# A hybrid backbone on one core: the end of layer 0 and the start of layer 1 done by token segments

## The chip, the core and the metric

The kernel runs on one core of a Trainium2 chip. The metric is device time in microseconds (us), the median of several executions. A core has a matrix engine (TensorE, PE in the profile; its weight loads are shown as PEld), a vector engine (VectorE, DVE), a scalar engine that evaluates functions (ScalarE, ACT), GpSimd (POOL) and a queue that issues transfers (SyncE, SP). Each engine works through its own list of instructions strictly in order and stops at an instruction whose inputs are not there.

## What is computed

The network is a two-layer trunk over 256 context tokens and 512 latent tokens with 1024 channels. Each layer has a normalised and modulated input, a mixer, and then a gated convolutional feed-forward network (FFN). Cut to what matters:

```python
def trunk_layer(x_lat, x_ctx, c, c_ctx, p, mixer, rope, need_ctx):
    m_lat = [m[:, None, :] for m in adaln_mods(c, p)]
    m_ctx = adaln_mods(c_ctx, p)
    o_ctx, o_lat = mixer(modulate(x_ctx, p['norm_mix_g'], m_ctx[0], m_ctx[1]),
                         modulate(x_lat, p['norm_mix_g'], m_lat[0], m_lat[1]), p, rope, need_ctx)
    x_lat = x_lat + m_lat[2] * o_lat
    x_lat = x_lat + m_lat[5] * conv_ffn(modulate(x_lat, p['norm_ffn_g'], m_lat[3], m_lat[4]), p)
    ...

def conv_ffn(h, p):
    u = dwconv_centred(h @ p['ffn_w_up'], p['ffn_conv_w'], p['ffn_conv_b'])
    gate, val = jnp.split(u, 2, axis=-1)
    return (jax.nn.silu(gate) * val) @ p['ffn_w_down']
```

`modulate` is an RMS norm over the 1024 channels of one token, times a gain and a scale, plus a shift. Layer 1's mixer is a Mamba-2 state-space part (`ssd`) beside windowed attention. Its input projection makes, among others, the 32 decay columns (`dt`) and the columns B and C (`bm`, `cm`), which go through a five-tap convolution and a silu.

## The kernel before, in words

Channels lie on the 128 partitions and tokens along the free axis, so an activation of all tokens is eight tiles of 128 x 768: 256 context columns and then 512 latent ones. `SEG2` lists the two segments, context first; the two token groups have different modulation, so every residual and every modulation is written per segment.

Every product is made in three passes to keep precision: a weight tile is split into a rounded high half (`whi`, a cast on ScalarE, line 325) and a low half (`wlo`, a subtraction on VectorE, or on GpSimd for the layer-1 input weights, line 326), the activation into `hi` and `lo` likewise, and `dense` adds hi*hi, lo*hi and hi*lo in one accumulator. One weight tile serves one output block of 128 channels. Raw weights arrive in two buffers (`NWR` = 2), the halves are kept in three (`NW` = 3): a raw buffer is loaded again once the low half of its tile is made, and a pair of halves is overwritten once the product that used it is done. `plan` lists all weight tiles in the order of use.

The FFN of layer 0 runs over four groups of hidden blocks (6, 6, 5, 5). For each group the `up` products make the hidden blocks, and then eight `down` products, one per output block `m` and here 5 blocks x 3 passes x 2 segments = 30 matmuls each, are added into the residual tiles `x` by `resid` (VectorE, line 484). After the last group comes layer 1's norm, `prenorm`: `sumsq` squares each `x` tile (ScalarE, line 429), adds the squares of tiles 0 to 6 on GpSimd (line 434), and sums over the partitions with a product by a matrix of ones; `rstd` makes the inverse root with Ln and Exp (lines 415 and 416, one function-table load in front of each); then, for each tile, u = x * gain * r (VectorE, line 462), the high half (ScalarE, line 463) and the low half (VectorE, line 477, for five tiles; lines 469 and 474 on ScalarE and GpSimd for the last three). The latents of `x` are also saved to memory (`sp_x`). Then `ada_group` (64 small matmuls for a later modulation), `decays` (the `dt` columns, a chain of functions and scans, a store `sp_ac` and its reload `E`, spread over all partitions), the two B blocks (dense, five-tap convolution, silu at line 1237, transposes at line 1243), the two C blocks (accumulator `sd`), and so on. `decays` and the first B block use the `by_pass` order: all eight hi*hi matmuls first, then lo*hi, then hi*lo.

The program is written tile by tile; a list scheduler then sets a fixed order for each engine, by its own costs and by the pools that tiles are taken from. What stands in those lists is therefore not the order of the text.

## Time and profile before

| What | us |
|---|---|
| Median of 3 runs (lowest, highest) | 2268.85 (2264.03, 2269.86) |
| The profiled execution's own time | 2264.21 |
| Its span, first to last instruction | 2262.3 |
| PE busy | 2076.5 (92%) |
| DVE busy | 1346.3 (60%) |
| ACT busy | 928.3 (41%) |
| POOL busy | 506.2 (22%) |

The shares are averages over stages with different limits, so the table only says that TensorE is the engine to follow. The stretch that the change touches lies between 1336 us, where the last eight down products of layer 0 begin, and about 1440 us, where TensorE takes up the transposes of the first B block; the views below are cut to it. In a row of the timeline stand the start, the length, engine, line, operation, output<-inputs, shapes and count, and in brackets the idle time before and what ended it. The three runs differ by 0.26%.

### The profile page before, as it was taken

To read this page: it belongs to the slowest core of one execution; us is meant where nothing else is said; L and a number is where in the kernel's file an instruction comes from. 1 tells how busy PE (TensorE), PEld (TensorE's weight loads), DVE (VectorE), ACT (ScalarE), POOL (GpSimd) and SP (SyncE) were. 2 spreads that over 40 slices of the span, in tenths; PEclk is the share of its full clock that TensorE was granted. 3 is DMA by queue.
4 is the path that set the end of the run, shared out by engine and by line. 5 is a ranking of instruction groups with operands and counts; after the bars stand their busy time and mean duration, and the time that the engine had idled before them with its cause. 6 is when DMAs were issued, how large, how long until landed. Compare 5 with 4: busy or idle time off the path is not lost.

```text
span 2262.3 us, 33884 instructions
## 1 busy us (share of the span) xinstructions
PE 2076.5 (92%) x13558; PEld 1640.9 (73%) x13558; DVE 1346.3 (60%) x2081; ACT 928.3 (41%) x1434; POOL 506.2 (22%) x486
## 2 busy tenths in 40 slices
PE   5888889788998999999999998898888999999997
PEld 3666667566654878888888886786565667888886
DVE  5566965666766465445354444678985556554555
ACT  4445663532355244233132335544344345342434
POOL 0027686611223010000000004442641230000000
PEclk9999999698999999999999999999889999999998
DMA  8477777669741441211212213213426032323231
GB/s 303 125 206 206 182 211 195 211 190 320 259 165 42 154 139 62 61 66 57 75 53 60 75 58 114 96 52 117 133 71 172 28 111 79 96 92 98 84 116 61
DMA packets 181069, 282.58 MB, mean 125 GB/s; under 512 B 63328, under 2 KB 118656, under 8 KB 177840
## 3 DMA queue, kind: packets, MB, share of 16 engines
q1 hardware_dynamic: 180912, 280.42, 40.6%
q8 instruction: 107, 1.75, 0.3%
q14 instruction: 50, 0.41, 0.1%
HBM read 225.43 MB, written 47.33 MB: 121 GB/s over the span
## 4 chain that ended last, share of the span: by engine, by line
PE 65%; DVE 6%; ACT 5%; DMA 5%; issue 3%; POOL 1%; SPq 0%; DVEq 0%; ACTq 0%; POOLq 0%
PE acc L267 49%; PE sd L267 3%; PE o L267 3%; PE wo L267 2%; PE ab L267 2%; PE b L267 2%; DMA u<-sp_v 1%; DVE E L1359 1%; DMA aw<-ada 1%; POOL I L750 1%; PE ax L267 1%; PE ad L267 1%; POOL w L748 1%; DMA E<-sp_ac 1%; ACT L416 1%
## 5 line engine op out<-in xcount | busy, mean ns | idle before, releaser
L267 PE MATMUL acc<-s,whi 128*128 128x512 f32 (+1 forms) x3104 | 759.8, 356 | 3.0 <-ACT s L463 3.0
L267 PEld LDWEIGHTS acc<-s,whi 128*128 128x128 f32 x3104 | 546.0, 188 | 97.3 <-ACT s L463 4.8
L267 PE MATMUL acc<-s,wlo 128*128 128x512 f32 (+1 forms) x1552 | 462.0, 358 | 0.0
L267 PE MATMUL acc<-h,whi 128*128 128x256 f32 (+2 forms) x1248 | 321.1, 371 | 15.9 <-ACT p L639 5.0
L325 ACT CAST whi<-wraw 128x1024 fp32r<-128x1024 f32 (+5 forms) x228 | 210.0, 923 | 282.3 <-PE acc L267 218.0
L267 PEld LDWEIGHTS acc<-s,wlo 128*128 128x128 f32 x1552 | 289.5, 188 | 42.9 <-DVE wlo L326 0.7
L267 PEld LDWEIGHTS acc<-h,whi 128*128 128x128 f32 (+1 forms) x1248 | 223.7, 197 | 68.4 <-issue 15.4
L326 DVE TENSOR_TENSOR wlo<-wraw,whi 128x1024 fp32r<-128x1024 f32 (+5 forms) x205 | 218.7, 1069 | 44.2 <-ACT whi L325 43.6
L381 DVE SCALAR_TENSOR_TENSOR s<-acc,pv,s 128x511 f32<-128x511 f32 (+1 forms) x132 | 87.0, 659 | 246.2 <-ACT s L380 245.4
L380 ACT ACTIVATE s<-acc,pv 128x512 f32<-128x512 f32 (+1 forms) x132 | 93.4, 708 | 235.4 <-PE acc L267 224.2
L484 DVE SCALAR_TENSOR_TENSOR x<-acc,mods,x 128x512 f32<-128x512 f32 (+1 forms) x136 | 79.4, 620 | 175.0 <-PE acc L267 174.8
L267 PE MATMUL acc<-h,wlo 128*128 128x256 f32 (+2 forms) x624 | 179.5, 362 | 0.0
L434 POOL TENSOR_TENSOR f<-f,f 128x768 f32<-128x768 f32 (+1 forms) x24 | 31.3, 1306 | 635.0 <-ACT f L429 625.1
L267 PEld LDWEIGHTS acc<-h,wlo 128*128 128x128 f32 (+1 forms) x624 | 119.3, 195 | 21.9 <-issue 5.6
L1178 POOL TENSOR_TENSOR s<-w,s 128x256 f32<-128x256 f32 x6 | 5.0, 855 | 381.3 <-ACT s L416 381.3
L383 DVE SCALAR_TENSOR_TENSOR s<-acc,pv,s 128x511 f32<-128x511 f32 (+1 forms) x132 | 87.2, 660 | 4.2
L750 POOL TENSOR_TENSOR I<-I,w 128x30 f32<-128x30 f32 (+14 forms) x120 | 76.7, 639 | 9.0
L748 POOL TENSOR_TENSOR w<-I 128x30 f32<-128x30 f32 (+14 forms) x120 | 69.4, 578 | 34.6 <-PE iv L267 25.8
L387 ACT CAST s<-s 128x768 fp32r<-128x768 f32 (+1 forms) x44 | 32.0, 727 | 106.1 <-DVE s L1151 106.1
L326 POOL TENSOR_TENSOR wlo<-wraw,whi 128x1024 fp32r<-128x1024 f32 x23 | 61.7, 2686 | 59.6 <-ACT whi L325 56.1
L1359 DVE TENSOR_SCALAR E<-E,acm 128x128 f32<-128x128 f32 x128 | 61.2, 546 | 14.6 <-ACT G L1356 14.6
L723 DVE TENSOR_TENSOR W<-gk,con 64x512 f32<-64x512 f32 x48 | 32.8, 683 | 51.2 <-ACT PB L722 47.3
(390 smaller groups left out, 3347.3 us busy)
## 6 DMA issues: line engine op xcount, KB each, us to landing
aw<-ada SPq DMA_DIRECT2D x96, 512.0 KB, 5.8
wraw<-up SPq DMA_DIRECT2D x88, 512.0 KB, 3.5
rec<-sp_rec SPq DMA_DIRECT2D x24, 1024.0 KB, 9.7
wraw<-w_in SPq DMA_DIRECT2D x47, 512.0 KB, 3.8
wraw<-down SPq DMA_DIRECT2D x40, 384.0 KB, 3.1
...
E<-sp_ac SPq DMA_DIRECT2D x16, 512.0 KB, 5.5
...
```

Of the source, the lines that this page charges most:

```text
L267: ins = nc.tensor.matmul(o, lhsT=lhsT, rhs=rhs, start=start, stop=stop, skip_group_check=shared)
L325: nc.scalar.copy(hi[:, :kt], raw[:, :kt])
L326: (eng or tt)(out=lo[:, :kt], in0=raw[:, :kt], in1=hi[:, :kt].bitcast(F32), op=ALU.subtract)
L380: act(o[rows, t0:t0 + n], ps[rows, po:po + n], AF.Identity, scale=w1, bias=b)
L381: stt(out=o[rows, t0 + 1:t0 + n], in0=ps[rows, po:po + n - 1], scalar=w0, in1=o[rows, t0 + 1:t0 + n], op0=ALU.mult, op1=ALU.add)
L383: stt(out=o[rows, t0:t0 + n - 1], in0=ps[rows, po + 1:po + n], scalar=w2, in1=o[rows, t0:t0 + n - 1], op0=ALU.mult, op1=ALU.add)
L387: nc.scalar.copy(hi, src)
L484: stt(out=x[:, t0:t0 + n], in0=ps[:, po:po + n], scalar=mods[:, c6 * 8 + m, c:c + 1], in1=x[:, t0:t0 + n], op0=ALU.mult, op1=ALU.add)
L723: tt(out=w[hk], in0=b[hk].rearrange("p c (a t) -> p c a t", a=2), in1=mk[hk].rearrange("p (a t) -> p a t", a=2).unsqueeze(1).to_broadcast( ...
L748: eng.tensor_tensor(out=tmp, in0=I[:, m + 1:, m:m + 1].to_broadcast([P, n, m]), in1=I[:, m:m + 1, :m].to_broadcast([P, n, m]), op=ALU.mult)
L750: eng.tensor_tensor(out=I[:, m + 1:, :m], in0=I[:, m + 1:, :m], in1=tmp, op=ALU.add)
L1359: ts(out=e[:, h], in0=e[:, h], scalar1=acm[:, c, h0 + h:h0 + h + 1], scalar2=0.0, op0=ALU.subtract, op1=ALU.min)
```

## The change

Only the end of layer 0 and the start of layer 1 are written differently.

- In the last group of layer 0's FFN the eight down products are made for the latents alone, then layer 1's norm of the latents is written (`tail`), then the eight down products for the context, and the norm of the context. Each of the eight weight tiles is therefore loaded and split twice (`plan` lists them twice).
- The sum of squares, the inverse root and the modulation are made per segment: twice as many instructions, each over 512 or 256 columns instead of one over 768 or two.
- `decays` and the first B block multiply the latents first, all 24 matmuls, and then the context (`by_seg`).
- The sixteen hi and lo input tiles of layer 0's FFN live in a pool `h1` outside the FFN's pool (which has 24 tiles now instead of 40), and layer 1's hi and lo tiles take the same sixteen.
- The saving of the latents (`sp_x`) is written after the latents' down products.

```diff
@@ plan_ffn
-            if layer == 0 or gsz > 4:
+            for _ in range(1 + (layer == 0 and j0 + gsz == FT)) if layer == 0 or gsz > 4 else ():
                 plan.extend(("down", a["down"][layer, m][:, j0:j0 + gsz], gsz) for m in range(8))
@@ dense
-        for i, (k, q) in enumerate(order):
+        steps = [(i, k, q, (g,)) for g in segs[::-1] for i, (k, q) in enumerate(order)] if by_seg else \
+            [(i, k, q, segs) for i, (k, q) in enumerate(order)]
+        for (i, k, q, sg_) in steps:
             wt, xt = passes[q]
-            for (po, t0, n, _) in segs:
+            for (po, t0, n, _) in sg_:
@@ ffn
-            return T("ffn", [P, width], "s", 40, dt)
+            return T("ffn", [P, width], "s", 40 if layer else 24, dt)
-        hh, hl = prenorm(xs, mods, f"norm_ffn_g{layer}", 3, 4, lambda: S(F32R), lambda k: S(), nsegs or segs,
+        hh, hl = prenorm(xs, mods, f"norm_ffn_g{layer}", 3, 4, lambda: S(F32R) if layer else row_tile("h1", "h", 16, F32R), lambda k: S(), nsegs or segs,
...
+            if tail is not None and j0 + gsz == FT:
+                for seg in segs[::-1]:
+                    for m in range(8):
+                        ps = acc()
+                        dense(ps, next_w("down"), P, us, ul, nk=gsz, segs=[seg])
+                        resid(xs[m], ps, mods, 5, m, [seg])
+                    tail(seg)
+                break
@@ after the FFN of layer 0
-    ffn(0, mods0, xs, SEG2, NTOK, "left", lambda: ada_group(1, 3, mods1, "aw2", 5))
     open_pool("h1", "left")
     xsp = tc.dram_tile([P, KT, NLAT], F32, name="sp_x")
-    for k in range(KT):
-        dma(xsp[:, k], xs[k][:, L0:L1])
-    hh, hl = prenorm(xs, mods1, "norm_mix_g1", 0, 1, lambda: row_tile("h1", "h", 16, F32R), lambda k: xs[k], add=ptt, npool=3)
+    hs1 = []
+    def norm1(seg):
+        if seg[1] == L0:
+            for k in range(KT):
+                dma(xsp[:, k], xs[k][:, L0:L1])
+            hs1.extend(row_tile("h1", "h", 16, F32R) for _ in range(16))
+        it = iter(hs1)
+        prenorm(xs, mods1, "norm_mix_g1", 0, 1, lambda: next(it), lambda k: xs[k], [seg], add=ptt, npool=3)
+    ffn(0, mods0, xs, SEG2, NTOK, "left", lambda: ada_group(1, 3, mods1, "aw2", 5), tail=norm1)
+    hh, hl = hs1[:8], hs1[8:]
@@ decays
-        dense(ps, next_w("cd"), 64, hh, hl, by_pass=True)
+        dense(ps, next_w("cd"), 64, hh, hl, by_pass=True, by_seg=True)
@@ the two B blocks
-        dense(ps, next_w("cd"), P, hh, hl, by_pass=True)
+        dense(ps, next_w("cd"), P, hh, hl, by_pass=True, by_seg=g == 0)
```

Where the change adds lines, all later line numbers rise: 325 and 326 stay, 484 (`resid`) becomes 486, 462 becomes 464, 477 becomes 479, 1237 becomes 1256, 1356 and 1361 become 1375 and 1380.

**TensorE, the first three down products.** In both kernels the scheduler runs three products up to the last hidden block (tiles `s_1178x`, which come late) and finishes them afterwards. Before, products 0 and 1 (accumulators `acc_11784`, `acc_11823`) are finished while most of product 2 (`acc_11862`) still lies ahead:

```order
L267 MATMUL acc_11784<-s_11781,whi_11657 128x256
L267 MATMUL acc_11784<-s_11781,whi_11657 128x512
L267 MATMUL acc_11823<-s_11780,wlo_11720 128x256
L267 MATMUL acc_11823<-s_11780,wlo_11720 128x512
L267 MATMUL acc_11823<-s_11781,whi_11719 128x256
L267 MATMUL acc_11823<-s_11781,whi_11719 128x512
L267 MATMUL acc_11862<-s_11391,whi_11787 128x256
L267 MATMUL acc_11862<-s_11391,whi_11787 128x512
```

Now (products 0, 1 and 2 of the latents are `acc_11788`, `acc_11811`, `acc_11834`; product 3 is `acc_11857`):

```order
L267 MATMUL acc_11834<-s_11784,whi_11791 128x512
L267 MATMUL acc_11834<-s_11784,wlo_11792 128x512
L267 MATMUL acc_11788<-s_11785,whi_11661 128x512
L267 MATMUL acc_11811<-s_11785,whi_11723 128x512
L267 MATMUL acc_11834<-s_11785,whi_11791 128x512
L267 MATMUL acc_11857<-s_11264,whi_11814 128x512
L267 MATMUL acc_11880<-s_11264,whi_11837 128x512
L267 MATMUL acc_11857<-s_11264,wlo_11815 128x512
```

The three products now end in three consecutive matmuls, and the next matmuls need the next two weight tiles.

**VectorE, the last down products.** Before, low halves and residuals alternate, and the u of layer 1's norm (line 462) begin when all residuals are done:

```order
L326 TENSOR_TENSOR wlo_11944<-wraw_11941,whi_11943 128x640
L484 SCALAR_TENSOR_TENSOR x_7153<-acc_11940,mods_6_75,x_7153 128x256
L484 SCALAR_TENSOR_TENSOR x_7153<-acc_11940,mods_6_75,x_7153 128x512
L326 TENSOR_TENSOR wlo_11983<-wraw_11980,whi_11982 128x640
L484 SCALAR_TENSOR_TENSOR x_7154<-acc_11979,mods_6_75,x_7154 128x256
L484 SCALAR_TENSOR_TENSOR x_7154<-acc_11979,mods_6_75,x_7154 128x512
L484 SCALAR_TENSOR_TENSOR x_7155<-acc_12018,mods_6_75,x_7155 128x256
```

Now, in the context's products, the low halves of the weight tiles of products 5 and 7 (`wlo_12128`, `wlo_12174`) stand behind the latents' norm. In front of `wlo_12128` are eight u over 512 columns (the first and the last are shown), in front of `wlo_12174` five low halves of activations (`h_11988` to `h_11992`):

```order
L326 TENSOR_TENSOR wlo_12105<-wraw_12102,whi_12104 128x640
L486 SCALAR_TENSOR_TENSOR x_7151<-acc_12101,mods_6_75,x_7151 128x256
L464 SCALAR_TENSOR_TENSOR x_7149<-x_7149,gs_11996,f_12025 128x512
...
L464 SCALAR_TENSOR_TENSOR x_7156<-x_7156,gs_11996,f_12025 128x512
L326 TENSOR_TENSOR wlo_12128<-wraw_12125,whi_12127 128x640
L486 SCALAR_TENSOR_TENSOR x_7152<-acc_12124,mods_6_75,x_7152 128x256
L486 SCALAR_TENSOR_TENSOR x_7153<-acc_12147,mods_6_75,x_7153 128x256
L326 TENSOR_TENSOR wlo_12151<-wraw_12148,whi_12150 128x640
L479 SCALAR_TENSOR_TENSOR h_11988<-x_7149,mods_7_76,h_11980 128x512
...
L479 SCALAR_TENSOR_TENSOR h_11992<-x_7153,mods_7_76,h_11984 128x512
L486 SCALAR_TENSOR_TENSOR x_7154<-acc_12170,mods_6_75,x_7154 128x256
L326 TENSOR_TENSOR wlo_12174<-wraw_12171,whi_12173 128x640
```

The u and the low halves of the latents have moved in between two products' weights.

**ScalarE, the silu of the first B block.** Its output is `f_12450` before and `f_12539` now; TensorE's transposes wait for it. The tiles `G` and `E` belong to the decays (exponentials of the reloaded decay sums, four tiles of each at this place). Before, it stands behind the third G:

```order
L1356 ACTIVATE G_13037<-E_13035 128x1024
L1356 ACTIVATE G_13059<-E_13057 128x1024
L1356 ACTIVATE G_13115<-E_13113 128x1024
L1237 ACT_TABLE_LOAD
L1237 ACTIVATE f_12450<-f_12450 128x768
```

Now it stands behind four G, four E and what lies between them; from the third G on:

```order
L1375 ACTIVATE G_13204<-E_13202 128x1024
L1375 ACTIVATE G_13226<-E_13224 128x1024
L1249 ACTIVATE f_12619<-acc_12564,pv_71 128x256
L325 CAST whi_12647<-wraw_12645 128x1024
L1380 ACTIVATE E_13146<-E_13146 128x1024
L1380 ACTIVATE E_13202<-E_13202 128x1024
L1380 ACTIVATE E_13224<-E_13224 128x1024
L1249 ACTIVATE cf_12675<-sd_12644,pv_71 128x512
L325 CAST whi_12685<-wraw_12683 128x1024
L1256 ACT_TABLE_LOAD
L1256 ACTIVATE f_12539<-f_12539 128x768
```

Eight instructions have come in between the third G and the silu with its table load.

More of the change, by code (lines that the diff above doesn't have):

```diff
@@ L363, in hybrid_kernel, with dense @@
     SEGX = [(0, 0, NLAT, 0)]
-    def dense(ps, w, m, xhi, xlo, k0=0, nk=8, segs=SEG2, first=True, last=True, kx=0, by_pass=False):
+    def dense(ps, w, m, xhi, xlo, k0=0, nk=8, segs=SEG2, first=True, last=True, kx=0, by_pass=False, by_seg=False):
         hi, lo = w
```

2 lines of the change are left out of this document (1 added, 1 removed).

## The prediction

> **What bounds the kernel now.** I read the stretch by stages first (windows of the kernel before: length, then busy time of PE, PEld, DVE, ACT, POOL, granted clock, DMA share, GB/s), then the waits in the timeline of TensorE.
>
> ```profile
> 1336.00:1378.10 42.10, 42.09 (x240) 36.61 (x238) 16.78 (x26) 14.22 (x18) 16.02 (x8) 1.00 0.36 116
> 1378.10:1406.90 28.80, 23.13 (x152) 14.43 (x153) 20.51 (x33) 18.18 (x30) 8.50 (x6) 0.94 0.30 106
> 1406.90:1431.50 24.60, 24.60 (x129) 20.13 (x127) 12.16 (x20) 10.74 (x13) 7.22 (x3) 1.00 0.25 76
> 1431.50:1440.10 8.60, 0.03 (x2) 0.02 (x1) 4.95 (x23) 5.16 (x6) 0.01 (x1) 0.64 0.70 246
> ...
> 1377.57 0.52 PE L267 MATMUL acc<-s,whi 128*128 128x256 f32 x2
> 1378.28 1.56 PE L267 MATMUL acc<-f,ones 128*128 128x256 f32 x4 [0.19 <-POOL f L434]
> 1440.08 0.90 PE L1243 MATMUL b<-con,f 128*128 128x128 f32 x3 [8.57 <-ACT f L1237]
> ```
>
> The 240 matmuls of the last down products fill 42.1 us without a gap. Then come 28.8 us of norm, with TensorE partly idle, until the decays' product is done (1406.9), and then 24.6 full us. At 1431.5 TensorE stops for 8.57 us, and what it waits for is the silu of the first B block (L1237). So the norm's gap is not all: whatever arrives earlier at 1406.9 must also bring that silu forward. What holds the silu is seen on ScalarE, VectorE and the queue:
>
> ```profile
> 1407.06 0.90 ACT L1253 ACTIVATE f<-acc,pv 48x768 f32<-48x768 f32 x1 [3.77 <-PE acc L267]
> 1413.86 0.98 DVE L1257 SCALAR_TENSOR_TENSOR f<-f,f 48x768 f32<-48x768 f32 x1 [8.13 <-ACT f L1256]
> 1419.13 0.34 SPq L1265 DMA_DIRECT2D sp_ac<-f  x1
> 1431.29 1.06 ACT L1356 ACTIVATE G<-E 128x1024 f32<-128x1024 f32 x1 [6.12 <-DMA E<-sp_ac]
> 1436.82 1.06 ACT L1356 ACTIVATE G<-E 128x1024 f32<-128x1024 f32 x1 [1.72 <-DMA E<-sp_ac]
> 1437.89 1.28 ACT L1237 ACT_TABLE_LOAD   x1
> 1439.19 0.84 ACT L1237 ACTIVATE f<-f 128x768 f32<-128x768 f32 x1
> ```
>
> From the decays' product to the store of their sums: 1419.13 - 1406.9 = 12.2 us. From there to TensorE's restart: 1440.08 - 1419.13 = 20.9 us, of which 12.2 until the first reloaded E tile and 5.5 more until the third. The silu's own input was long ready; it stands behind three G in ScalarE's list.
>
> **The change part by part.** TensorE's work hardly changes. The end of layer 1 shows 512-column matmuls in front of 132 with 256 columns and a weight tile each:
>
> ```profile
> 2223.22 0.39 PE L267 MATMUL acc<-s,wlo 128*128 128x512 f32 x1
> 2223.45 0.62 PE L267 MATMUL acc<-s,whi 128*128 128x512 f32 x2
> 2223.91 0.40 PE L267 MATMUL acc<-s,wlo 128*128 128x512 f32 x1
> 2224.37 15.13 PE L267 MATMUL acc<-s,w 128*128 128x256 f32 x132
> ```
>
> Three of 512 take 0.69 us, 0.23 each; one of 256 takes 15.13 / 132 = 0.115. The loads of weights stay hidden. The down products are 120 x 0.23 + 120 x 0.115 = 41.4 us, 0.7 less than now. The cost is in what feeds them:
>
> ```profile
> L484 DVE SCALAR_TENSOR_TENSOR x<-acc,mods,x 128x512 f32<-128x512 f32 x8 | 5.9, 741 | 0.0
> 1386.29 8.56 DVE L462 SCALAR_TENSOR_TENSOR x<-x,gs,f 128x256 f32<-128x256 f32 x16 [7.02 <-ACT f L416]
> L326 DVE TENSOR_TENSOR wlo<-wraw,whi 128x640 fp32r<-128x640 f32 x5 | 4.0, 817 | 1.7 <-ACT whi L325 1.7
> L325 ACT CAST whi<-wraw 128x640 fp32r<-128x640 f32 x5 | 3.6, 729 | 13.9 <-PE acc L267 10.7 <-DMA wraw<-down 3.2
> 1383.20 0.90 ACT L415 ACTIVATE f<-acc,epsc 128x768 f32<-128x768 f32 x1 [1.65 <-PE acc L267]
> 1385.41 0.84 ACT L416 ACTIVATE f<-f 128x768 f32<-128x768 f32 x1
> wraw<-w_in SPq DMA_DIRECT2D x9, 512.0 KB, 3.7
> wraw<-down SPq DMA_DIRECT2D x8, 320.0 KB, 2.9
> ```
>
> The eight pairs of u (256 and 512 columns) take 8.56 us, so about 0.67 for 512 and 0.40 for 256 back to back; I take the same for residuals and low halves of activations. I count from the start of the down products (1336).
>
> (a) The first three products now end together, at 45 x 0.23 = 10.4. VectorE then owes three residuals (3 x 0.67) and a low half (0.82) before product 3 can go on: 12.8. TensorE has two matmuls meanwhile. Wait 2.0. The other latent products end at 29.6; their weights come in time (a raw tile lands 2.9 us after issue, a product lasts 3.45).
>
> (b) The latents' sum of squares: two products by ones, about 1.0 each (1.56 us above covers 768 columns), now between the context's products 0 and 1. The sum is there at 34.6, Ln done 35.2, a square, a cast and the table load 37.65, Exp 38.25. All this hides behind the context's products 1 to 4, which end at 40.2.
>
> (c) Product 5 needs `wlo_12128`, behind eight u: 38.25 + 8 x 0.67 = 43.6, two adds of GpSimd in between (1.2, see below) 44.8, the low half 45.6. TensorE waits 5.3 us.
>
> (d) Product 7 needs `wlo_12174`: behind a residual pair, a low half, five low halves of activations (3.35) and one more residual: 51.9. Here GpSimd has five operations of its own, and the trace shows what that does to VectorE:
>
> ```profile
> 1395.10 2.02 DVE L477 SCALAR_TENSOR_TENSOR h<-x,mods,h 128x256 fp32r<-128x256 f32 x1
> 1397.70 2.06 DVE L477 SCALAR_TENSOR_TENSOR h<-x,mods,h 128x256 fp32r<-128x256 f32 x1
> 1403.37 0.74 DVE L477 SCALAR_TENSOR_TENSOR h<-x,mods,h 128x512 fp32r<-128x512 f32 x1
> 1394.98 1.86 POOL L474 TENSOR_TENSOR h<-x,h 128x768 fp32r<-128x768 f32 x1 [13.01 <-ACT x L469]
> 1397.62 3.82 POOL L474 TENSOR_TENSOR h<-x,h 128x768 fp32r<-128x768 f32 x2 [0.78 <-ACT x L469]
> ```
>
> A 256-column low half takes 2.0 us while a GpSimd operation runs, and a 512-column one 0.74 afterwards: such VectorE operations wait out GpSimd's. At 1.86 us per 768 columns the five (three of 512, two of 256) are 5.0 us. So 0 to 5 is added; I take the middle, since some of it falls on residuals that read the accumulator. Product 7 starts at 54.4 and ends at 56.0.
>
> Sum of the down stage: 56.0 - 42.1 = **+13.9** (11.4 to 16.4).
>
> (e) From there to the end of the decays' product now stand 14.7 us: residual and square 1.0; ScalarE's two casts of 1.0, two table loads of 1.28, Ln and Exp (0.4 each), and about 0.7 for the wait for the second cast's load (3.7 us after its buffer is free): 8.1; eight u 3.3; five low halves 2.1, GpSimd's collisions 1.0; the last matmuls 0.2. All latent matmuls of the decays and 20 of the 64 for the modulation lie inside. Against 28.8: **-14.1** (-12.8 to -15.3). So (a) to (d) eat what the norm gives.
>
> (f) From there to the store: one cast of 1.05 us less in ScalarE's list, one copy of 0.4 more on VectorE: **-0.6**.
>
> (g) From the store to the silu:
>
> ```profile
> E<-sp_ac SPq DMA_DIRECT2D x4, 512.0 KB, 8.7
> 1440.60 0.77 ACT L1230 ACTIVATE cf<-sd,pv 128x512 f32<-128x512 f32 x1
> 1445.24 1.99 ACT L1361 ACTIVATE E<-E 128x1024 f32<-128x1024 f32 x2
> ```
>
> G tiles start 2.77 us apart, so the fourth E lands at about 12.2 + 3 x 2.77 = 20.5 us after the store. Then one after another: G 1.06, a convolution start 0.55, a cast 1.0, three E at 0.95, one of 0.7, a cast 0.95, a table load 1.28, the silu 0.84: 29.7 against 20.9. **+8.7**. If E4 landed with E3, it would be +5.9; if the E also waited for VectorE's subtractions, +10.
>
> (h) TensorE fills 1.5 us of that wait with nine matmuls of the next block: **-1.4** if its work is what counts later. The blocks that use these E and G stand 2.9 us of matmuls later behind the transposes than before; if they count, +2.9 in its place.
>
> To the restart it is 13.9 - 14.1 - 0.6 + 8.7 = 7.9 later, so 6.5 or 10.8 with (h). The later stretch says which is nearer (window, then TensorE's wait there):
>
> ```profile
> 1520.00:1680.00 160.00, 131.16 (x828) 103.01 (x829) 139.80 (x280) 63.04 (x75) 75.81 (x35) 0.88 0.33 108
> 1552.58 0.69 PE L267 MATMUL sd<-E,xtm 128*64 128x128 f32 x2 [8.37 <-DVE E L1364]
> ```
>
> VectorE is 139.8 of 160 us busy and TensorE waits for its E, but not throughout: I take the middle, **+8.5**. Against the profiled execution (2264.2; 1.9 of it outside the span) that is 2272.7; the median of the runs is 4.6 above that execution, so 2277.
>
> The clock:
>
> ```profile
> 1440.00:1442.00 2.00, 1.92 (x7) 1.73 (x8) 1.27 (x4) 2.00 (x4) 0.61 (x1) 0.50 0.00 0
> 1444.00:1446.00 2.00, 2.00 (x12) 1.77 (x12) 1.62 (x3) 2.00 (x4) 0.76 (x1) 0.97 0.12 29
> ```
>
> After the wait of 8.57 us TensorE ran about 4 us at 0.50. My sum has one such price, product 5 after its wait, 14 x 0.115 more, and there the low half of product 7 is later anyway. [...]
>
> **The rivals.** *The weights are not late* (A). If VectorE reached both low halves in time, the down stage would be +3.1 (2.0 of (a), 1.8 of the ones, less 0.7): 8.5 - 10.8 = -2.3, 2266.5, not slower. For it speaks that VectorE is busy 16.8 of 42.1 us there now; against it, its fixed list. It decides if product 5 starts at 40.3.
>
> *A, and the later stretch gives back* (B). With the E made earlier, the wait of 8.37 us could vanish as well: -10.7, 2258. Against it: the E tiles of the next blocks are reloaded only when TensorE has used these.
>
> *The forecast, but the later stretch absorbs a good part* (C): 5.5 of the same 8.37 us, +3.0, 2272. For it: TensorE has 2.9 us more to do before that point.
>
> *Cold clock* (D): two extra prices as in the 4 us at 0.50, 1.7 each, on top: +11.9, 2281. Speaks for it: the waits of (c) and (d) are 5.3 and up to 4 us.
>
> **How the numbers follow.** Forecast 0.42 (own range 2271 to 2284 by the bounds of (d), (e), (g), (h)), A 0.20, B 0.13, C 0.15, D 0.10. 0.3% is 6.8 us, about what these runs can tell from no change. Slower by more: two thirds of the forecast, nearly all of D, a little of C: 0.42. Faster by more: B and a little of A: 0.18. The rest, 0.40, is within. The range 2260 to 2287 leaves out most of B and the tail of D.
>
> **What would show it.** (a): TensorE's wait of about 2 us for VectorE after 45 matmuls. (c): about 5 us for the low half with eight u ahead of it. (d): low halves of 2 us beside GpSimd. (e): 13 to 16 us from the last down matmul to the decays' end. (g): the silu 9 us later behind the store, and a wait of TensorE of 7 to 11 us. Wrong if the context's products run without a gap, or if TensorE restarts at the transposes earlier than 1440.

## The result and the profile after

The changed kernel takes **2279.21 us** (median of 5 runs, 2278.74 to 2280.84). The kernel before, run beside it, takes 2268.22 (5 runs, 2264.03 to 2269.86). The ratio is **1.0051, 95% interval 1.0040 to 1.0062**: by the ratio 11.6 us slower (9 to 14), by the medians 11.0. The profiled executions have spans of 2277.4 and 2262.3 us; 1.6 us of these 15.1 lie ahead of the changed stretch.

First the stages of the kernel after, cut as the prediction cut those of before (columns: length, then busy time of PE, PEld, DVE, ACT, POOL with their instructions, granted clock, DMA share, GB/s).

```profile
1337.40:1398.10 60.70, 48.13 (x246) 40.58 (x245) 40.12 (x48) 30.88 (x49) 21.80 (x16) 0.93 0.40 121
1398.10:1415.50 17.40, 14.56 (x94) 8.64 (x92) 6.00 (x15) 10.54 (x20) 8.33 (x6) 0.84 0.44 140
1415.50:1447.70 32.20, 32.20 (x183) 25.05 (x181) 16.28 (x46) 16.08 (x19) 4.78 (x2) 1.00 0.42 133
1447.70:1456.80 9.10, 3.14 (x10) 2.34 (x9) 8.33 (x17) 7.10 (x9) 4.56 (x2) 0.70 0.18 58
```

The down products took 42.1 us without a gap; they now take 60.7, of which TensorE works 48.1. The norm behind them shrank from 28.8 to 17.4 us. From the decays' product to the transposes it is now 41.3 us (33.2 before). So the transposes of the first B block start 119.4 us behind the first down product, 15.3 later than the 104.1 of before.

The waits of TensorE in that stretch, in the timeline of the kernel after (start, length, engine, line, operation; in brackets the wait and what ended it):

```profile
1348.49 0.47 PE L267 MATMUL acc<-s,whi 128*128 128x512 f32 x1 [0.47 <-DVE x L486]
1350.44 0.50 PE L267 MATMUL acc<-s,wlo 128*128 128x512 f32 x1 [0.83 <-DVE wlo L326]
1383.24 0.58 PE L267 MATMUL acc<-s,wlo 128*128 128x256 f32 x1 [4.83 <-DVE wlo L326]
1394.78 0.58 PE L267 MATMUL acc<-s,wlo 128*128 128x256 f32 x1 [6.25 <-DVE wlo L326]
1403.01 3.21 PE L267 MATMUL acc<-h,whi 128*64 128x512 f32 x8 [2.66 <-ACT f L417]
1452.66 0.98 PE L267 MATMUL acc<-h,whi 128*128 128x256 f32 x2 [4.94 <-DVE f L1253]
1456.82 0.90 PE L1262 MATMUL b<-con,f 128*128 128x128 f32 x3 [1.05 <-ACT f L1256]
```

Two waits of 4.83 and 6.25 us are for the low half of a weight tile that is loaded for the second time. What VectorE does ahead of these low halves, and GpSimd beside it, stands in the timeline of the same kernel:

```profile
1376.10 6.35 DVE L464 SCALAR_TENSOR_TENSOR x<-x,gs,f 128x512 f32<-128x512 f32 x8 [0.73 <-ACT f L418]
1382.37 0.81 DVE L326 TENSOR_TENSOR wlo<-wraw,whi 128x640 fp32r<-128x640 f32 x1
1385.12 8.48 DVE L479 SCALAR_TENSOR_TENSOR h<-x,mods,h 128x512 fp32r<-128x512 f32 x5
1393.92 0.81 DVE L326 TENSOR_TENSOR wlo<-wraw,whi 128x640 fp32r<-128x640 f32 x1
1383.23 3.11 POOL L476 TENSOR_TENSOR h<-x,h 128x512 fp32r<-128x512 f32 x2 [4.64 <-DVE wlo L326]
1390.27 2.78 POOL L326 TENSOR_TENSOR wlo<-wraw,whi 128x1024 fp32r<-128x1024 f32 x1
...
L479 DVE SCALAR_TENSOR_TENSOR h<-x,mods,h x5: 1209/1759/2822, 1385.1 to 1390.8; 128x512 fp32r<-128x512 f32 x5
1408.12 2.06 DVE L479 SCALAR_TENSOR_TENSOR h<-x,mods,h 128x256 fp32r<-128x256 f32 x5
```

Eight u stand in front of the first (6.35 us), five low halves of activations in front of the second (8.48 us). The grouped row gives shortest, median and longest of these five in ns: 1209, 1759 and 2822, where such an operation took 741 alone. GpSimd works at the same time, and the longest one falls beside GpSimd's own weight tile of 2.78 us.

Then the way from the decays to the silu, in the timelines of ScalarE and of SP's queue:

```profile
1415.59 0.90 ACT L1272 ACTIVATE f<-acc,pv 48x768 f32<-48x768 f32 x1 [5.53 <-PE acc L267]
1426.81 0.34 SPq L1284 DMA_DIRECT2D sp_ac<-f  x1
1438.82 1.06 ACT L1375 ACTIVATE G<-E 128x1024 f32<-128x1024 f32 x1 [8.44 <-DMA E<-sp_ac]
1445.63 1.06 ACT L1375 ACTIVATE G<-E 128x1024 f32<-128x1024 f32 x1 [0.28 <-DMA E<-sp_ac]
1455.93 0.84 ACT L1256 ACTIVATE f<-f 128x768 f32<-128x768 f32 x1
```

From the store to the restart it is 1456.82 - 1426.81 = 30.0 us (20.9 before), because ScalarE's list has more in front of the silu.

Last, how the start of layer 1 goes on. The windows of before (from the start of the down products) and of after, in pieces of the same length:

```profile
1336.00:2262.30 926.30, 855.33 (x4414) 670.20 (x4412) 571.81 (x951) 392.75 (x574) 200.65 (x120) 0.96 0.30 95
1336.00:1420.00 84.00, 78.32 (x467) 62.32 (x466) 43.18 (x67) 39.48 (x56) 29.33 (x15) 0.98 0.32 107
1420.00:1560.00 140.00, 122.64 (x728) 101.66 (x727) 101.26 (x217) 69.68 (x94) 55.59 (x30) 0.93 0.22 74
1560.00:1720.00 160.00, 131.62 (x762) 101.11 (x761) 129.91 (x243) 70.46 (x87) 66.22 (x31) 0.89 0.46 130
1720.00:1870.00 150.00, 146.24 (x702) 98.35 (x701) 79.36 (x126) 60.53 (x122) 43.82 (x37) 0.99 0.26 89
```

```profile
1337.40:2277.40 940.00, 861.43 (x4415) 673.63 (x4413) 582.88 (x959) 402.13 (x595) 203.81 (x129) 0.96 0.31 96
1337.60:1421.60 84.00, 68.60 (x378) 52.47 (x376) 46.31 (x64) 47.02 (x75) 32.51 (x23) 0.92 0.41 127
1421.60:1561.60 140.00, 134.01 (x802) 112.14 (x802) 96.70 (x194) 64.45 (x90) 49.41 (x28) 0.96 0.26 82
1561.60:1721.60 160.00, 127.07 (x745) 98.18 (x744) 134.63 (x263) 68.72 (x81) 71.51 (x35) 0.89 0.35 113
1721.60:1871.60 150.00, 143.34 (x636) 92.52 (x636) 81.05 (x124) 62.76 (x120) 40.56 (x32) 0.98 0.27 82
```

TensorE's idle time is the length less its busy time. It goes from 5.7 to 15.4 us in the first 84 us, from 17.4 to 6.0 in the next 140, from 28.4 to 32.9 in the next 160 and from 3.8 to 6.7 in the next 150. Over the whole rest of the program it is 71.0 before and 78.6 after (+7.6), and TensorE is 6.1 us longer busy with as many matmuls, at a mean granted clock of 0.96 in both. So the stretch loses 9.7 us of idle time early, wins 11.4 back in the next piece, where it had waited before, and loses 7.4 of these again.

### The profile page after: what moved, and what is told of

Same layout as the page of the kernel before. It is cut to its first block, busy times and chain, and to the rows that moved or that the text cites. A ratio compares the mean times of both kernels' runs of the same rounds, so it can differ in the third digit from the quotient of the medians.

```text
span 2277.4 us, 33952 instructions
## 1 busy us (share of the span) xinstructions
PE 2082.9 (91%) x13558; PEld 1644.6 (72%) x13558; DVE 1357.9 (60%) x2091; ACT 937.3 (41%) x1455; POOL 509.0 (22%) x495
## 4 chain that ended last, share of the span: by engine, by line
PE 65%; DVE 7%; DMA 5%; ACT 5%; issue 2%; POOL 1%; SPq 1%; DVEq 0%; ACTq 0%; POOLq 0%
PE acc L267 49%; PE o L267 3%; PE sd L267 3%; PE b L267 3%; PE wo L267 2%; PE ab L267 2%; DVE E L1378 2%; DMA aw<-ada 1%; DMA E<-sp_ac 1%; PE ax L267 1%; PE ad L267 1%; POOL I L752 1%; DMA rec<-sp_rec 1%; POOL w L750 1%; PE gk L267 1%
## 5 line engine op out<-in xcount | busy, mean ns | idle before, releaser
L267 PE MATMUL acc<-h,whi 128*128 128x256 f32 (+2 forms) x2656 | 617.1, 352 | 33.6 <-ACT f L1436 8.9
L267 PEld LDWEIGHTS acc<-h,whi 128*128 128x128 f32 (+1 forms) x2656 | 460.9, 192 | 115.8 <-issue 18.3
L267 PE MATMUL acc<-s,whi 128*128 128x512 f32 (+1 forms) x1696 | 468.8, 373 | 2.4 <-ACT s L465 1.7
L267 PE MATMUL acc<-h,wlo 128*128 128x512 f32 (+2 forms) x1328 | 358.9, 351 | 0.0
L267 PEld LDWEIGHTS acc<-s,whi 128*128 128x128 f32 x1696 | 309.4, 190 | 62.9 <-ACT s L465 2.2
L267 PE MATMUL acc<-s,wlo 128*128 128x512 f32 (+1 forms) x848 | 290.7, 374 | 11.9 <-DVE wlo L326 11.9
L267 PEld LDWEIGHTS acc<-h,wlo 128*128 128x128 f32 (+1 forms) x1328 | 249.3, 191 | 38.7 <-issue 7.4
L267 PEld LDWEIGHTS acc<-s,wlo 128*128 128x128 f32 x848 | 161.1, 190 | 43.4 <-DVE wlo L326 13.4
L436 POOL TENSOR_TENSOR f<-f,f 128x256 f32<-128x256 f32 (+2 forms) x30 | 34.3, 1142 | 645.4 <-ACT f L431 636.4
L1253 DVE SCALAR_TENSOR_TENSOR f<-acc,pv,f 128x510 f32<-128x510 f32 (+3 forms) x80 | 49.0, 614 | 27.6 <-ACT f L1249 26.0
```

The source lines that it names most:

```text
L267: ins = nc.tensor.matmul(o, lhsT=lhsT, rhs=rhs, start=start, stop=stop, skip_group_check=shared)
L436: add(out=sq[:, n0:n1], in0=prev[:, n0:n1], in1=sq[:, n0:n1], op=ALU.add)
L1253: stt(out=o[:, t0 + lo:t0 + hi], in0=ps[:, po + lo + s:po + hi + s], scalar=col(f"sconv_w{tap}", j), in1=o[:, t0 + lo:t0 + hi], op0=ALU.mu ...
```

## Experiments

The profiled executions differ ahead of the changed stretch even where their programs are the same there (by 4.6 us between the changed kernel and e1). So I count from one instruction there, the last product of silu and value of the last hidden group (VectorE, about 4 us behind the start of the last down products). Of each profiled execution the table gives, in us behind it: the last residual of the down products, the end of the decays' product, the store of their sums, the start of the first B block's transposes, the first product with an E, and the end of the program. The last columns are the timed runs against runs of the kernel before beside them, whose medians lie between 2267.63 and 2269.28.

| Kernel | last residual | decays' product | store | transposes | first E product | end | ratio [95%] | median us (runs) |
|---|---|---|---|---|---|---|---|---|
| before | 39.3 | 67.0 | 79.1 | 100.1 | 189.4 | 922.3 | | 2268.22 (5) |
| after | 57.1 | 74.0 | 85.2 | 115.2 | 206.6 | 935.8 | 1.0051 [1.0040, 1.0062] | 2279.21 (5) |
| e1_keep_weights | 51.4 | 67.2 | 78.2 | 104.5 | 194.9 | 930.1 | 1.0034 [1.0023, 1.0046] | 2275.16 (6) |
| e2_no_gpsimd_lows | 56.2 | 73.1 | 84.3 | 115.1 | 206.3 | 935.1 | 1.0047 [1.0032, 1.0061] | 2278.99 (4) |
| e3_silu_first | 58.6 | 75.6 | 86.8 | 100.6 | 203.0 | 933.9 | 1.0048 [1.0030, 1.0066] | 2277.78 (4) |
| e4_silu_first_before | 39.2 | 67.0 | 79.1 | 90.5 | 193.8 | 925.3 | 0.9996 [0.9987, 1.0006] | 2268.19 (10) |
| e5_lows_late | 56.9 | 70.6 | 81.8 | 107.1 | 198.3 | 934.9 | 1.0061 [1.0045, 1.0078] | 2280.63 (4) |
| e6_apply_after_downs | 43.5 | 71.6 | 83.5 | 108.3 | 197.3 | 928.0 | 1.0040 [1.0026, 1.0054] | 2275.25 (6) |
| e7_apply_after_keep | 43.1 | 64.5 | 76.9 | 97.9 | 195.9 | 927.4 | 1.0026 [1.0015, 1.0037] | 2274.13 (10) |
| e8_norm_parts_only | 39.3 | 67.1 | 78.1 | 102.2 | 192.8 | 927.9 | 1.0028 [1.0013, 1.0044] | 2274.68 (10) |
| e9_more_tensor_work | 39.3 | 67.0 | 79.1 | 100.8 | 198.6 | 934.8 | 1.0043 [1.0026, 1.0059] | 2279.55 (5) |
| e10_more_vector_work | 39.3 | 67.0 | 79.1 | 100.4 | 200.7 | 935.5 | 1.0047 [1.0032, 1.0062] | 2281.01 (4) |
| e11_buffers_only | 39.2 | 67.1 | 79.1 | 100.6 | 189.9 | 925.9 | 0.9998 [0.9986, 1.0010] | 2269.37 (10) |
| e12_apply_after_keep_no_gpsimd | 43.6 | 64.7 | 76.6 | 103.0 | 192.0 | 921.6 | 0.9994 [0.9984, 1.0003] | 2268.24 (10) |

e11 has the order of before past the anchor and still ends 3.6 us later in its profile: differences below about 4 us in the column of the end say nothing, and verdicts go by the ratios.

**e1: no second load of the weights.** On the changed kernel, six of the eight weight tiles are split once and kept for the context's products.

```diff
+NRE = 2
-    plan.extend(("down", ..., gsz) for m in range(8))
+    plan.extend(("down", ..., gsz) for m in range(NRE if layer == 0 and j0 + gsz == FT else 8))
...
-    dense(ps, next_w("down"), P, us, ul, nk=gsz, segs=[seg])
+    if m < NRE:
+        w = next_w("down")
+    elif m not in kept:
+        raw = T("sb", [P, 8, P], "wraw", NWR)
+        dma(raw[:, :gsz], a["down"][layer, m][:, j0:j0 + gsz])
+        w = [S(F32R)[:, :gsz * P].rearrange("p (k c) -> p k c", c=P) for _ in range(2)]
+        split(w[0], w[1], raw[:, :gsz])
+        kept[m] = w
+    else:
+        w = kept[m]
+    dense(ps, w, P, us, ul, nk=gsz, segs=[seg])
```

> The changed kernel, but six of the eight tiles of the last down weights (products 2 to 7) stay on chip in both halves from the latents' pass, so the context's products 2 to 7 need no reload, no cast and no low half. In the changed kernel's trace TensorE waits 4.8 us and 6.2 us for such low halves (products 5 and 7 of the context), and runs at half rate behind each wait. Theory of the prediction, terms (c) and (d): both waits go; the down stage shrinks from 60.5 us to 47 to 50 (a wait of about 3 us for a free accumulator stays, since VectorE's residuals stand behind its eight u). VectorE's five low halves of activations (8.5 us) still stand ahead of the last two residuals, so the context's norm comes only about 5 us earlier: 2279 - 5 = 2274, between 2270 and 2276. Rival, the late weights are the whole loss: the norm comes 11 to 13 us earlier, 2267. Rival, the later stretch absorbs it: 2279, with the waits moved behind the decays.

It takes 2275.16 us. Its timeline around the context's last product:

```profile
1389.05 5.18 PE L268 MATMUL acc<-s,s 128*128 128x256 f32 x30 [3.39 <-DVE x L487]
1389.70 7.17 DVE L480 SCALAR_TENSOR_TENSOR h<-x,mods,h 128x512 fp32r<-128x512 f32 x5
1396.79 0.86 DVE L487 SCALAR_TENSOR_TENSOR x<-acc,mods,x 128x256 f32<-128x256 f32 x2
```

The two waits for weights are gone, so their cause is the second load in VectorE's list. A new wait takes their place, 3.39 us for a residual that frees an accumulator, and the last two residuals stand behind the same five low halves, 7.17 us here. The last residual comes 5.7 us earlier than in the changed kernel, and about 4 us of the 11.6 are gone by the ratios, though their intervals overlap a little. The norm work in VectorE's list delays whatever stands behind it, weights or residuals.

**e2: no low halves on GpSimd for the latents.** All eight are made by VectorE.

```diff
-        prenorm(xs, mods1, ..., [seg], add=ptt, npool=3)
+        prenorm(xs, mods1, ..., [seg], add=ptt, npool=0 if seg[1] == L0 else 3)
```

> The changed kernel, but all eight low halves of the latents are VectorE's and none GpSimd's (one line). Theory of (d): the five that took 8.5 us on VectorE wait out GpSimd's operations; without GpSimd's three, eight take 8 x 0.75 = 6.0 us, or up to 7.5 where a low half of a weight is still GpSimd's; product 7's weight comes 1 to 2.5 us earlier and the whole is 1 to 3 us faster, 2276 to 2278. Rival, the 1.7 us is what such an operation takes: eight take 13.6 us, product 7 is 5 us later and the kernel 5 us slower, 2284.

It takes 2278.99 us, as the changed kernel does; the 1 to 3 us that were expected did not come. The grouped row of the eight low halves, and the one GpSimd operation left beside them:

```profile
L479 DVE SCALAR_TENSOR_TENSOR h<-x,mods,h x8: 739/741/2823, 1385.3 to 1390.9; 128x512 fp32r<-128x512 f32 x8
1390.69 2.44 POOL L326 TENSOR_TENSOR wlo<-wraw,whi 128x1024 fp32r<-128x1024 f32 x1 [3.62 <-ACT whi L325]
1394.47 0.58 PE L267 MATMUL acc<-s,wlo 128*128 128x256 f32 x1 [5.49 <-DVE wlo L326]
```

At least half of the eight take 0.74 us, the longest 2.82, and that one runs beside GpSimd's weight tile. So this VectorE operation, 0.74 us alone, waited out GpSimd's of 2.44; without GpSimd's three additions eight low halves take 8.4 us (from 1385.3 to 1390.9 + 2.8), as five did with them. It does not pay here, since VectorE then has three more to do itself: the wait falls from 6.25 to 5.49 only.

**e3 and e4: the silu of the first B block ahead of the decays' weights and the G,** on the changed kernel (e3) and on the one before (e4). It takes out step (g) of the prediction.

```diff
     def decays(): ...
-        tt(out=wgt, in0=dec, in1=acm, op=ALU.subtract)
-        act(wgt, wgt, AF.Exp)
-        tt(out=wgt, in0=wgt, in1=dtm, op=ALU.mult)
-        act(dec, dec, AF.Exp)
...
+    def weights(after):
+        with tc.issue_after(after):
+            tt(out=wgt, in0=dec, in1=acm, op=ALU.subtract)
+        with tc.issue_after(silu[0].ins):
+            act(wgt, wgt, AF.Exp)
+            act(dec, dec, AF.Exp)
+        tt(out=wgt, in0=wgt, in1=dtm, op=ALU.mult)
...
-                act(gc, e, AF.Exp)
+                with tc.issue_after(silu[0].ins):
+                    act(gc, e, AF.Exp)
```

`weights` is called behind the convolution of the first B block.

> The changed kernel, but on ScalarE the four G behind the decays, and the two small Exp of the decays' weights, are issued only after the silu of the first B block, and on VectorE the subtraction that waits for the decays' reload only after that block's convolution. Theory of (g): the silu (1455.9 in the changed kernel) comes at about 1440, TensorE's waits of 4.9 and 1.0 us and the half rate behind them (about 8 us at half, so 4) go, and the kernel is 6 to 10 us faster, 2269 to 2273. Rival, the later stretch decides (the G and E are then 3 us later, and VectorE is 36 of 40 us busy from 1540 on): between 2276 and 2281.

> The same edit on the kernel before: G, the two small Exp and the subtraction behind the first B block's silu and convolution. There the silu's input was long ready and TensorE waited 8.57 us, with about 4 us at half rate behind it. Theory of (g): TensorE's wait falls below 2 us and the kernel is 7 to 10 us faster, 2258 to 2261. Rival, the later stretch decides: 2266 to 2271, with longer waits for E between 1540 and 1680.

The transposes start 14.6 us earlier in e3 and 9.6 earlier in e4, and the end moves by less than the noise: 2277.78 us against 2279.21, and a ratio of 0.9996 for e4. The timeline of TensorE in e4 shows waits that it did not have before:

```profile
1449.01 0.90 PE L1246 MATMUL b<-con,f 128*128 128x128 f32 x3 [5.69 <-ACT btm L1247]
1453.40 1.01 PE L267 MATMUL acc<-h,whi 128*128 128x256 f32 x2 [2.20 <-DVE f L1236]
1615.92 0.79 PE L267 MATMUL acc<-h,whi 128*128 128x512 f32 x1 [4.49 <-ACT f L1427]
```

Right behind the restart TensorE waits 5.69 us for the copy of the transposes, which on ScalarE stands behind the G, and 2.20 for a convolution: 7.9 of the 8.57 us have only moved. So **an earlier restart of TensorE at the transposes does not by itself bring the end of the program forward.** It is not shown that the wait, taken away without a substitute, would be worth nothing: the edit moves the G and the decays' weights back, and in e4 the first product with an E comes 4.4 us later than before (in e3 3.6 us earlier than in the changed kernel). The times are those of the rival that the later stretch decides, in both kernels; the longer waits for E between 1540 and 1680 that it named for e4 did not come (10.5 us in all in that stretch, counted from the anchor, where it was 16.2).

**e5: the latents' low halves behind the context's down products.** They are kept in a list and written ahead of the context's norm.

```diff
-                stt(out=lo[:, s], in0=us[k][:, s], ...)
+                def low(lo=lo, k=k, s=s, c=c):
+                    stt(out=lo[:, s], in0=us[k][:, s], ...)
+                low() if late is None else late.append(low)
...
+        if seg[1] != L0:
+            for low in lows:
+                low()
```

> The changed kernel, but the latents' low halves are written behind the context's products in the program. On VectorE and TensorE the order up to the decays stays the changed kernel's; what differs is the interleaving from the heads' state updates on, which is again nearly that of the kernel before (the changed kernel's own had moved: fewer matmuls of the next blocks between the state updates, and a wait of 8.9 us at 1612 to 1621 that before does not have). Theory now, from the trace of after: the change loses 13.8 us up to TensorE's restart and part of the end's loss is that moved interleaving; with it undone 3 to 8 us come back, 2271 to 2276. Rival, the later stretch gives the same time by either interleaving: 2277 to 2281.

The waits of the down stage stay (the last residual at 56.9), the decays come 3.4 us earlier than in the changed kernel and the transposes 8.1. It takes 2280.63 us, no less. So neither these 3.4 us of the decays nor the order in which the later blocks are interleaved, which is here close to the one of before, explains the loss.

**e6: all norm work but the sums behind the last residual.** The sums of squares and the inverse roots stay per segment; u, high and low halves wait for the last residual, the latents first.

```diff
-        prenorm(xs, mods1, ..., [seg], add=ptt, npool=3)
+        (_, t0, n, _) = seg
+        rs[t0] = rstd(sumsq(xs, [seg], ptt), D, 0, t0, n, seg[0])
+        if t0 == L0:
+            return
+        for sg in SEG2[::-1]:
+            it = iter(hs1)
+            with tc.issue_after(last[0].ins):
+                prenorm(xs, mods1, ..., [sg], npool=NP1, r=rs[sg[1]])
```

`last[0]` is the last residual's instruction, and `NP1` is 3 as before.

> The changed kernel, but the latents' norm only takes its sum and its Exp during the context's products; the eight u and the low halves stand behind the last residual of the context on VectorE. Theory of (c) and (d): TensorE's waits of 4.8 and 6.2 us go, since no low half of a weight stands behind a u any more; the down stage is 43 to 46 us instead of 60.7 (before: 42.1). Behind it VectorE needs 16 x 0.4 to 0.8 for the u and 10 x 0.4 to 0.75 for the low halves, up to 5 more for GpSimd's collisions: the decays' product is done 62 to 68 us after the start of the down products (after 78.2, before 70.9). If that reaches the end: 2279 - 12 = 2267, between 2263 and 2270, as fast as the kernel before or faster. Rival, the later stretch absorbs it: above 2272.

The down stage loses its waits, as the theory has it: the last residual is at 43.5 instead of 57.1. But the decays' product ends at 71.6, later than in the kernel before, and the kernel takes 2275.25 us. VectorE and GpSimd behind the last residual, in the timeline of e6:

```profile
1388.76 10.66 DVE L465 SCALAR_TENSOR_TENSOR x<-x,gs,f 128x512 f32<-128x512 f32 x16
1399.34 5.37 DVE L480 SCALAR_TENSOR_TENSOR h<-x,mods,h 128x512 fp32r<-128x512 f32 x10
1385.98 2.35 POOL L327 TENSOR_TENSOR wlo<-wraw,whi 128x1024 fp32r<-128x1024 f32 x1 [0.55 <-ACT whi L326]
1388.83 2.89 POOL L327 TENSOR_TENSOR wlo<-wraw,whi 128x1024 fp32r<-128x1024 f32 x1
1398.22 8.76 POOL L327 TENSOR_TENSOR wlo<-wraw,whi 128x1024 fp32r<-128x1024 f32 x1 [6.50 <-ACT whi L326]
1406.94 5.86 POOL L477 TENSOR_TENSOR h<-x,h 128x512 fp32r<-128x512 f32 x6
```

A weight tile that GpSimd splits in 2.35 us takes 8.76. VectorE's run ends at 1399.34 + 5.37 = 1404.7, and GpSimd's tile 2.27 us behind that, at 1406.98: its own length. So GpSimd stood until VectorE's whole run was through, and its six low halves came after. It is not always so: the tile before, at 1388.83, got through beside the same run in 2.89 us, and there VectorE was the later one: its 16 u took 10.66 us, against 8.56 in e7, where GpSimd began only at 1396.03. That the decays are late because of GpSimd is not shown: TensorE shows no wait for it, and from 1393.1 until the decays' product is done (1414.3) it works 21.1 of 21.2 us, at a mean clock of 0.88 and with matmuls of the first B block in between.

**e7: e6 and e1 together,** and **e12: the same with `NP1 = 0`,** so that VectorE makes all 16 low halves.

> The edit of the kernel with the u and low halves behind the last residual, and the one with six weight tiles kept on chip, together: VectorE has six low halves less (4.9 us) and the queue six reloads less. Theory that VectorE's work is what counts: 2 to 5 us faster than the edit alone. Theory that only TensorE's waits count: no difference (within 2 us), since these low halves then lie beside TensorE's products.

> The kernel with the u and low halves behind the context's last residual and with six weight tiles kept, now with all sixteen low halves on VectorE and none on GpSimd. In that kernel's trace GpSimd's first of six took 7.0 us beside VectorE's low halves (1.7 alone), all six 11.6, and the decays' product waited for them. Theory of the collision, seen from GpSimd's side: VectorE takes 5 us more, ends at 80.6 - 16 = about 61 us behind the anchor, and the decays' product is done 61 to 63 us behind the anchor, 1.5 to 3.5 us earlier; the whole 2270 to 2273. Rival, the later stretch gives it back: 2274 to 2276.

e7 takes 2274.13 us. Against e6 that is 1.1 less, which the intervals do not tell apart. GpSimd's low halves in e7, in the grouped view:

```profile
L478 POOL TENSOR_TENSOR h<-x,h x6: 733/1003/7032, 1396.0 to 1406.9; 128x512 fp32r<-128x512 f32 x3, 128x256 fp32r<-128x256 f32 x3
```

The first takes 7.03 us, the median 1.0: again GpSimd stands beside a run of VectorE. (The 1.7 us alone of the expectation for e12 is not shown: in the changed kernel such an operation took 1.72 us, at 1387.45, beside VectorE's low halves.) TensorE waits only 0.79 us for these low halves. In e12 the low halves, the first 84 us and the stretch up to the end of the decays' product are:

```profile
L481 DVE SCALAR_TENSOR_TENSOR h<-x,mods,h x16: 472/610/745, 1397.3 to 1405.4; 128x512 fp32r<-128x512 f32 x8, 128x256 fp32r<-128x256 f32 x8
1340.80:1424.80 84.00, 80.87 (x479) 63.08 (x479) 47.69 (x84) 44.14 (x68) 26.02 (x19) 1.00 0.38 117
1393.70:1409.50 15.80, 15.80 (x95) 10.30 (x96) 12.53 (x27) 6.40 (x14) 0.00 (x0) 1.00 0.16 65
```

None of the 16 is stretched, TensorE is idle for 3.1 us only (5.7 before, 15.4 after) and the granted clock is 1.00. e12 takes 2268.24 us: the loss is gone, and nothing is won. That was less than I had expected of the decays (64.7 where I had 61 to 63) and more of the end. VectorE was through at 1405.8, 61 us behind the anchor as expected (the expectation prints this as 80.6 - 16, which is 64.6), but TensorE had no idle time from 1393.7 on, so its own matmuls ended the decays' product. By the ratios the loss goes 11.6 us (changed kernel), 9.1 (e6), 5.9 (e7), -1.4 (e12). The step from e7 to e12 is outside both intervals, yet the decays end at the same time in both (64.5 and 64.7) and the transposes even later in e12. Behind them the first product with an E comes 3.9 us earlier in e12; why, and where the rest of the 7 us is won, no run says.

**e8: the norm alone per segment.** The down products go as before, both segments in one, with each weight tile loaded once; only the norm is written for the latents and then for the context.

```diff
+                for m in range(8):
+                    ps = acc()
+                    dense(ps, next_w("down"), P, us, ul, nk=gsz, segs=segs)
+                    resid(xs[m], ps, mods, 5, m, segs)
                 for seg in segs[::-1]:
-                    for m in range(8):
-                        ps = acc()
-                        dense(ps, next_w("down"), P, us, ul, nk=gsz, segs=[seg])
-                        resid(xs[m], ps, mods, 5, m, [seg])
                     tail(seg)
```

> One part of the change alone: the down products run as before, context and latents together, each weight once; only the norm goes by segments, latents first, and the decays' and the first B block's product too. Theory: no weight is late, the down stage is 42 to 43 us; behind it come the latents' sum and Exp (8 us), eight u of 0.75, five low halves (4 to 8 with GpSimd's collisions), the context's eight u and five low halves (5.4): 25 to 28 us against before's 28.8, so between 2264 and 2269, no change that can be told. Rival, the split itself costs (two sums, two table switches, 256 and 512 columns apart): slower than 2271.

From the last residual to the decays' product it is 67.1 - 39.3 = 27.8 us, where it was 67.0 - 39.3 = 27.7. Norm and first product by segments, with the down products as they were, win nothing by themselves. The kernel takes 2274.68 us, with runs from 2264.17 to 2281.38, so 6 us slower with a wide interval (3 to 10). The transposes come 2.1 us later. The trace shows one long new wait of TensorE behind the down products:

```profile
1390.53 2.07 PE L267 MATMUL acc<-f,ones 128*128 128x256 f32 x4 [6.86 <-POOL f L436]
```

GpSimd adds the context's squares only after the latents' part, and TensorE's sum of them waits. In the first 84 us TensorE is idle for 10.7 us, 5.0 more than before, though the decays' product ends on time. That is near the 6 us; no run takes this wait away by itself.

**e9 and e10: what work in the later stretch costs,** on the kernel before. e9 makes the first x block's product twice (48 matmuls more, 24 x 0.23 + 24 x 0.115 = 8.3 us of TensorE), e10 the convolutions of the first two x blocks twice (16 operations of VectorE more, 10.3 us of its time).

```diff
-            dense(ps, next_w("cd"), P, hh, hl)
+            w = next_w("cd")
+            for _ in range(2 if j == 0 else 1):
+                dense(ps, w, P, hh, hl)
```

```diff
     def conv5(o, ps, j, segs):
-        for (po, t0, n, _) in segs:
+        for (po, t0, n, _) in segs * (2 if j < 2 else 1):
```

> The kernel before, with the product of the first head block in the later stretch computed twice into the same accumulator (the first result is overwritten): 48 matmuls of 256 and 512 columns more, 48 x 0.174 = 8.4 us on TensorE at about 1460, where TensorE runs without a wait until 1544. Theory that TensorE's time counts wherever it is lost: +8, 2274 to 2277. Rival, the later stretch is elastic there: the wait of 8.4 us for VectorE's E at 1552 swallows most of it, 2267 to 2271.

> The kernel before, with the convolutions of the first two head blocks computed twice (the second overwrites the first): 16 operations of VectorE more, 4 x 0.51 + 4 x 0.77 for each block, 10.3 us in all, and 2.7 us of ScalarE, between 1460 and 1480, where VectorE is 22 of 40 us busy. Theory that TensorE's time counts: hidden but for what delays an accumulator, 0 to +4, 2268 to 2272. Rival, VectorE's work is the bound of the later stretch: +8 to +10, 2276 to 2278.

e9 costs 9.8 us (5.9 to 13.4) and e10 10.7 (7.3 to 14.1). Both count in full. e9's matmuls lie where TensorE has next to no gap (19.6 of 20 us busy between 1460 and 1480 before). In e10 the timeline of TensorE shows one new wait at the doubled convolution:

```profile
1469.94 0.98 PE L267 MATMUL acc<-h,whi 128*128 128x256 f32 x2 [8.74 <-DVE f L1234]
```

So both put 8 to 9 us on TensorE at one place, and the idle time behind it (28.4 us of TensorE and 30.1 of VectorE in the 160 us from 1560 on) gives none of it back. That fits a chain through both engines in turn, in which work on either delays the other; e4's wait that mostly moved fits it as well. What work added behind 1560 would cost was not tried.

**e11: only the tiles kept.** The kernel before with the changed pools: the layer-0 FFN takes its input tiles from those of layer 1, and its own pool is smaller.

```diff
-            return T("ffn", [P, width], "s", 40, dt)
+            return T("ffn", [P, width], "s", 40 if layer else 24, dt)
-    ... lambda: S(F32R), ...
+    ... lambda: S(F32R) if layer else row_tile("h1", "h", 16, F32R), ...
+    open_pool("h1", "left")
     ffn(0, mods0, xs, SEG2, NTOK, "left", ...)
-    open_pool("h1", "left")
```

> One part of the change alone on the kernel before: layer 0's feed-forward input lies in the pool of layer 1's h tiles, opened earlier, and its own pool has 24 instead of 40 tiles. Both theories: no more than 1 us, 2266 to 2270. Rival, the new places or their release cost time before the last down products (the changed kernel's start of them is 1.4 us later): 2269 to 2272 with that start over 1 us later than in the runs beside it.

The ratio is 0.9998: the buffers cost and win nothing. The difference comes from the rest of the change.

## Why the prediction was right, and where it was not

The time (2277 for 2279.21), the sign and the mechanism of the first stage were right; two terms were mis-sized, and the reason for which the early loss was taken to reach the end was not borne out. That the end came out within 3 us is partly luck: the restart came 7.4 us later than forecast, and the later stretch passed on less than all of it, which no term of the sum held. Counted from the start of the down products, 1336.0 before and 1337.4 after:

| Step | Forecast | Measured |
|---|---|---|
| (a) wait behind the first three products | 2.0 | 0.5 + 0.2 + 0.8 = 1.5 |
| (b) the latents' inverse root done at | 38.25 | 38.7 |
| (c) wait for the low half behind eight u | 5.3 | 4.83 |
| (d) product 7 starts at | 54.4 | 57.4 |
| down stage | +13.9 (11.4 to 16.4) | +18.6 |
| (e) to the end of the decays' product | -14.1 (-12.8 to -15.3) | -11.4 |
| (f) to the store | -0.6 | -0.9 |
| (g) to TensorE's restart | +8.7 | +9.1 |
| restart | +7.9 | +15.3 |
| end of the program | +8.5 | +13.7 in the two profiles, +11.0 between the medians |

**(a), (b), (c)** held, and e1 shows their cause: with the weights kept, the waits are gone.

**(d) failed by size.** Product 7 starts 3.0 us later than the sum had it. The five low halves were put at 3.35 + 2.5 = 5.85 us and took 8.48; e2 shows that GpSimd stretches them. The sum counted GpSimd's additions but not the weight tile that it splits at the same time, beside which one low half took 2.82 us. Residuals, which read the accumulator, were not longer beside GpSimd: 0.74 us at 1360.81 beside an addition of 1.34. The eight u of (c) fitted: with GpSimd's two adds they were put at 5.4 + 1.2 = 6.6 us and took 6.35.

**The clock** was priced once and had to be paid more often. The windows of after behind TensorE's waits:

```profile
1383.00:1386.40 3.40, 3.16 (x15) 3.17 (x16) 3.40 (x5) 2.64 (x7) 3.17 (x3) 0.52 0.39 104
1394.70:1398.10 3.40, 3.32 (x15) 3.33 (x16) 0.42 (x2) 0.42 (x1) 1.40 (x2) 0.50 0.64 214
1403.00:1407.00 4.00, 3.99 (x11) 2.17 (x12) 2.28 (x6) 3.22 (x6) 2.14 (x1) 0.57 0.58 166
1452.60:1460.60 8.00, 6.89 (x22) 5.64 (x23) 6.52 (x11) 7.11 (x10) 3.84 (x3) 0.50 0.30 105
```

Product 7 ran at 0.50 and lasted 3.3 us instead of 1.6; with the 3.0 of its late start this is the whole excess of the down stage, 18.6 - 13.9 = 4.7. That is the mechanism of rival D, inside the forecast's chain. Both waits for weights, of 4.83 and 6.25 us, were followed by a clock of 0.52 and 0.50, and a wait of 2.66 us by 0.57 (at 1403.0).

**(e) failed by 2.7 us**, since another engine ended it. The sum followed VectorE to the last low half, and VectorE was done at 1408.12 + 2.06 = 1410.2, 12.1 us behind the down stage where the sum had 14.5. (The parts that it names for residual, square and ScalarE make 7.1 us, not the 8.1 that it adds.) But TensorE could take up the decays' latents only at 1403.0, when ScalarE's Ln (L417) had read the accumulator of the squares, began at 0.57 of the clock, and then worked to 1415.5. The matmuls that the sum took to lie inside the norm were themselves the chain. No run tested this by itself.

**(f) and (g)** held as times from the store, but of the wait of 7 to 11 us that was named for TensorE only 4.94 + 1.05 = 6.0 came, the longer part for a convolution of VectorE. And (g) did not matter by itself: e3 takes it away and 14.6 us of the restart with it, and the time stays. The step from the restart to the end of the program was the weak one. The forecast took the middle between two sums, and both were sums of the restart. That an early loss reaches the end at all fits e9 and e10, in which the later stretch gives back nothing of 8 to 9 us lost between 1460 and 1480. But the loss is not simply the early idle time of TensorE: in e7 TensorE is idle for 3.4 of its first 84 us, less than the 5.7 of before, and yet e7 is 5.9 us slower.

**The rivals.** A and B, weights in time, fell by the waits of 4.83 and 6.25 us. C, the later stretch absorbs 5.5 us, is not the net effect, though its mechanism exists: idle time falls from 17.4 to 6.0 us in the 140 us behind the stage, and 7.4 of these 11.4 us are given back in the next 310. D names two more clock prices; the one of product 7 was paid. Its 1.7 us for each is an estimate that no run shows as a fixed price; measured are 3.3 us at a clock of 0.50 for product 7, where the sum had 1.6. Its 2281 lies as near to 2279.21 as the forecast's 2277, so the time does not tell the two apart.

What stays open: by what path the early loss reaches the end, whether e8's 6 us are its one wait, and where e12 wins 7 against e7 behind the decays. The table gives a hint: the loss goes with the first product with an E rather than with the transposes. Where that product comes at 189 to 194 us (before, e4, e11, e12) nothing is lost, but for e8 with 192.8; where it comes at 194.9 or later, every kernel is slower by 0.26% or more. That is an order among 14 kernels and not a test; no run moves that product alone. No version tried beats the kernel before.
